# One hybrid decoder block on one core: token tile 0 runs ahead of tiles 1 to 3, tile 1 also gathers its rows of u, and the dense u products come before the dense v products

## The chip, the core and the metric

The kernel runs on one core of a Trainium2 chip. A core has five engines with separate instruction queues: PE (TensorE, matrix multiplies and transposes), DVE (VectorE), ACT (ScalarE), POOL (GpSimd) and SP (SyncE, which issues DMAs here). Sixteen DMA engines move data between HBM and the on-chip memory SBUF; matrix products land in the accumulators of PSUM (eight banks). The metric is the time of one execution on the device, in microseconds, as the median of several runs.

## What is computed

One layer for 512 tokens of width 2048, in float32. Cut to what matters:

```python
z = rmsnorm(x) @ w_in                       # 2048 -> about 6150 columns
att = forgetting_attention(...)             # 8 heads x 128, causal
cell = mlstm_chunkwise(...)                 # 4 heads, chunks of 128 tokens, state carried on
x = x + concat(headnorm(att), headnorm(cell)) @ w_out
# PEER, for each token:
q = rmsnorm(x) @ w_q                        # 8 heads x 2 halves x 128
scores = q . keys                           # 8 heads x 2 x 128 keys
idx, gate = top 16 of the 16 x 16 sums of the two halves' top 16, softmax   # of 16384 experts
act = gelu(u[idx] . x) * gate               # 128 rows of u for each token
x = x + sum over the 128 of act * v[idx]
out = rmsnorm(x)
```

The attention and the mLSTM are causal: the mixer of the first 128 tokens needs nothing of the later ones.

## The kernel before

The tokens are four tiles of 128 (P). Weights come from HBM in **chunks** of 128x1024 float32 (512 KB). `stream_split` (L101) loads a chunk into one of three `raw` buffers, ACT casts it into a `hi` part (L109) and DVE forms the remainder `lo` (L111); a `raw` buffer is free once `lo` is formed. A float32 product is three matmuls: hi by hi, hi by lo, lo by hi.

`project_nat` (L118) has 128 tokens as the stationary operand and 512 weight columns moving; `project_t` (L136) has 128 weight columns stationary and all tokens moving, 512 of them in the mixer. So a chunk serves 24 matmuls of 512 columns for four tiles. The order is: norm of all four tiles, mixer of all four tiles (`mlstm_pair`, `fox_pair`, both over `range(NT)`), `w_out` for tiles 0 and 1, then for tiles 2 and 3, with tile 0's norm, queries (`w_q0`, 256 columns moving) and expert choice as steps beside them.

Then PEER has two paths. **Tile 0 gathers**: for each of its 128 slots (8 heads by 16), an indirect DMA on POOL's queue (L588) brings one row of u for each token, 128x2048 (1 MB), into one of three `row` buffers, and one DVE instruction forms the dot product (L603, called a dot below); after the activation, 128 more gathers bring rows of v, which DVE adds up (L614). `advance(n)` moves this series on by n steps at the places where it is written; each gather also waits for the last `hi` cast traced before it, so it is spread over the kernel. **Tiles 1 to 3 are dense**: for every one of 128 blocks of 128 experts (two chunks of `uT`), `dense_steps` forms gelu(u x) for 384 tokens (`sacc`, 48 matmuls of 384 columns), and for 16 groups of 8 blocks the products with v are summed (`y`, 512 columns moving). Gates enter as a table [block, key, token] that is built 32 tokens at a time (L878 to L901: DVE forms one-hot rows `o`, PE multiplies them into `gp`, ACT copies them into `stg`, and a DMA stores them in `gtab`); `load_gates` reads one group of all twelve tables, and `gated` (L938) multiplies and splits into `wbuf`.

68 of the u blocks (NEARLY) run beside the expert choice and the tables, with their results stored in `stab`; the other 60 are formed in the v stage, between v groups. Instructions stand on each engine in an order that a scheduler fixes from the written order and priorities; every engine works through its own queue in that order, so an instruction that waits holds up all behind it on its engine.

Of the kernel before, what the change touches and what calls it, by code (L numbers as in the profile page):

```python
# [10 lines left out]
F32 = mybir.dt.float32  # L11
# [70 lines left out]
def block_kernel(ctx: ExitStack, tc: tile.TileContext, a, out):  # L82
    nc = tc.nc

    const = ctx.enter_context(tc.tile_pool(name="const", bufs=1))
    stream = ctx.enter_context(tc.tile_pool(name="stream", bufs=2))
    cst = const.tile([P, C_KEEP], F32, name="cst")
# [30 lines left out]
    def project_nat(psA, src, parts, hook=None):  # L118
        """[tokens, 512 columns] of part.T @ w, one bank for each token tile."""
        acc = [psA.tile([P, 512], F32, tag="acc", name="acc") for _ in parts]  # L120
        for s in range(8):
            hi, lo = stream_split(src[s])
            for j, part in enumerate(parts):
                for kk in range(2):
                    kc = 2 * s + kk
                    xh, xl = part[:, 0, kc, :], part[:, 1, kc, :]
                    wh = hi[:, kk * 512:(kk + 1) * 512]
                    wl = lo[:, kk * 512:(kk + 1) * 512]
                    mm(acc[j], xh, wh, kc == 0, False)
                    mm(acc[j], xh, wl, False, False)  # L130
                    mm(acc[j], xl, wh, False, kc == KC - 1)
            if hook:
                hook()
        return acc

    def project_t(psA, src, xT):  # L136
        """[256 columns, tokens] of w.T @ xT, one bank for each 128 columns."""
        acc = [psA.tile([P, 512], F32, tag="acc", name="acc") for _ in range(2)]
        for s in range(4):
            hi, lo = stream_split(src[s])  # L140
            for j in range(2):
                for kk in range(4):
                    kc = 4 * s + kk
                    wh = hi[:, kk * 256 + j * P:kk * 256 + (j + 1) * P]
                    wl = lo[:, kk * 256 + j * P:kk * 256 + (j + 1) * P]
                    mm(acc[j], wh, xT[:, 0, kc, :], kc == 0, False)
                    mm(acc[j], wh, xT[:, 1, kc, :], False, False)
                    mm(acc[j], wl, xT[:, 0, kc, :], False, kc == KC - 1)
        return acc
# [15 lines left out]
    def transpose_split(psB, src, dst, groups=range(4)):  # L165
        """src [128 tokens, 2048] -> dst [128, hi/lo, kc, tokens]."""
        for g in groups:
            pt = psB.tile([P, 4, P], F32, tag="ps", name="pt")
            for k in range(4):
                kc = 4 * g + k  # L170
                nc.tensor.transpose(pt[:, k, :], src[:, kc * P:(kc + 1) * P], ident)
            h = dst[:, 0, 4 * g:4 * g + 4, :]
            nc.scalar.copy(out=h, in_=pt)  # L173
            nc.vector.tensor_tensor(out=dst[:, 1, 4 * g:4 * g + 4, :], in0=pt, in1=h.bitcast(F32), op=OP.subtract)

# [1 line left out]
    ssq = const.tile([P, NT, 4], F32, name="ssq")  # L177

    def add_block(sq, acc, t, n):
        """x2 block += acc, and its sum of squares."""  # L180
        xs = x2[:, t, n * 512:(n + 1) * 512]
        nc.vector.tensor_tensor(out=xs, in0=acc, in1=xs, op=OP.add)
        nc.scalar.activation(out=sq, in_=xs, func=AF.Square, accum_out=ssq[:, t, n:n + 1])

    def rstd_x2(pool, t):
        ss = pool.tile([P, 1], F32, tag="ss", name="ss", bufs=4)
        nc.vector.tensor_reduce(out=ss, in_=ssq[:, t, :], axis=AX.X, op=OP.add)
        return rstd_of(pool, ss, D, 1)

# [5 lines left out]
    with ExitStack() as mx:  # L195
        mc = mx.enter_context(tc.tile_pool(name="mc", bufs=1))
        xT = xtp.tile([P, 2, KC, S], F32R, name="xT")
        parts = [xT[:, :, :, t * P:(t + 1) * P] for t in range(NT)]
        with tc.tile_pool(name="n1", bufs=2) as n1:
# [14 lines left out]
            for t in range(NT):  # L214
# [7 lines left out]
                transpose_split(psB, hn, parts[t])  # L222
        cm = mc.tile([P, C_WID - C_MQK], F32, name="cm")
        nc.sync.dma_start(out=cm, in_=a["consts"][:, C_MQK:])
        bd = cm[:, C_BD - C_MQK:C_BD - C_MQK + S].rearrange("p (h t) -> p h t", h=MH)
        maskb = mc.tile([P, 3 * P], BF16, name="maskb")
        nc.vector.tensor_copy(out=maskb[:, 0:P], in_=ident)
        nc.vector.tensor_copy(out=maskb[:, P:], in_=cm[:, 0:2 * P])
        identb, mqkb, mstb = maskb[:, 0:P], maskb[:, P:2 * P], maskb[:, 2 * P:3 * P]
# [4 lines left out]

        mp = mx.enter_context(tc.tile_pool(name="mp", bufs=1))
        sp = mx.enter_context(tc.tile_pool(name="sp", bufs=2))
        mixed = x2

        # gates in rows: 0..7 fox forget, 32..35 mlstm input, 64..67 mlstm forget
        cF = mp.tile([104, S], F32R, name="cF")  # L240
        bF = mp.tile([104, S], F32, name="bF")
        erow = mp.tile([36, S], F32, name="erow")
        negM = mp.tile([36, S], F32, name="negM")
        cols = mp.tile([P, NT, 100], F32, name="cols")
        def gate_rows():
            # x2 is free until the mixer's first heads: 16 slots of 512 columns
# [5 lines left out]

            gps = psB.tile([P, 512], F32, tag="ps", name="gps")
            for s in range(2):
                ghi, glo = stream_split(a["w_gate"][s], 8 * 96)
                for kk in range(8):
                    kc = 8 * s + kk
                    wh, wl = ghi[:, kk * 96:(kk + 1) * 96], glo[:, kk * 96:(kk + 1) * 96]
                    mm(gps[:96], wh, xT[:, 0, kc, :], kc == 0, False)
                    mm(gps[:96], wh, xT[:, 1, kc, :], False, False)  # L260
                    mm(gps[:96], wl, xT[:, 0, kc, :], False, kc == KC - 1)
            g = slot(96, S)
            nc.scalar.activation(out=g, in_=gps[:96], func=AF.Identity, bias=gbias)
# [7 lines left out]
            # log1p(ex) = ln(u) + (ex - (u - 1)) / u  # L271
# [11 lines left out]
            # fox: F = cumsum(log_sigmoid), in two parts in rows 0.. and 32.. of cF, with ones in  # L283
            # rows 64.. and 96..; bF has ones against the parts and -F against the ones
# [8 lines left out]
            nc.vector.tensor_copy(out=bF, in_=cm[0:104, C_BASEF - C_MQK:C_BASEF - C_MQK + S])  # L293
# [16 lines left out]
            # running maximum M of e (from the state's), m = b + M  # L310
# [25 lines left out]
        def gate_cols(rowx, ones4, mprev, Mr):  # L336
            # columns: 0.. exp(-m), 32.. exp(m_prev - M), 64.. exp(e - M_last), 96.. exp(m_prev - M_last)
# [14 lines left out]
        qkp = mx.enter_context(tc.tile_pool(name="qkp", bufs=2))  # L352

        def w2k(shape, name):
            return sp.tile(shape, F32, tag="w2k", name=name, bufs=6)

        def w1k(shape, name):
            return sp.tile(shape, F32, tag="w1k", name=name, bufs=5)

        def col1(name):  # L360
            return sp.tile([P, 1], F32, tag=name, name=name)

# [1 line left out]
        def mlstm_pair(p2):  # L364
            qk = []
            for w in range(2):
                acc = project_t(psA, a["w_mqk"][p2][w], xT)
                dst = qkp.tile([P, 2, S], F32, tag="qk%d" % w, name="mqk")
                for j in range(2):
                    ci = w * 4 + p2 * 2 + j  # L370
                    cin = w2k([P, S + 3], "cin")
                    nc.vector.memset(cin[:, 0:3], 0.0)
# [694 lines left out]
```

## Time and profile before

| | |
|---|---|
| three runs | 3295.75, 3298.84 (median), 3302.25 us |
| profiled execution, first to last instruction | 3298.2 us |
| PE busy | 3245.6 us (98%) |
| DVE busy | 2293.9 us (70%) |
| ACT busy | 1242.8 us (38%) |
| POOL busy | 473.8 us (14%) |
| moved by DMA | 751.69 MB, mean 228 GB/s |

The profile is of one execution whose span is 0.6 us under the median. An engine's busy time is the union of its instructions' intervals. Matmuls are pipelined: one lasts longer than the distance to the next one's start, so what a series of them costs is read from the distance of their starts in the timeline, not from the mean duration.

### The profile page before, as it was taken

The numbers are of one execution on the slowest core, as the hardware profiler recorded it, in microseconds if no ns is written. First come the engines' busy times: TensorE is split into PE (matmuls) and PEld (weight loads), VectorE is DVE, ScalarE is ACT, GpSimd is POOL, SyncE is SP. The second block draws the span as 40 slices with busy tenths as digits, with TensorE's granted clock in tenths as the row PEclk, the third lists the DMA queues.
The fourth block names the chain that finished last, engine by engine and source line by source line (L and its number), as shares of the span: only waits on it lengthen the run. The fifth ranks groups of instructions, "written<-read, shape, count | busy, mean of one in ns | idle before, by whom it ended". The sixth has DMA issues, their size and how long they took to land.

```text
span 3298.2 us, 43394 instructions
## 1 busy us (share of the span) xinstructions
PE 3245.6 (98%) x16681; PEld 2886.8 (88%) x16681; DVE 2293.9 (70%) x3746; ACT 1242.8 (38%) x1667; POOL 473.8 (14%) x380
## 2 busy tenths in 40 slices
PE   8999999999999999999999999999999999999998
PEld 6788787778799999999998888888899899898997
DVE  5542324467888989988867778876777767677774
ACT  4432223355554444455533333333233233232333
POOL 0000000100112323200012211111211112122110
PEclk9999999999999999999999999999999999999999
DMA  4232232266657667676788888887787887777774
GB/s 149 77 90 83 77 96 71 84 228 198 218 166 250 232 244 259 231 252 223 252 319 301 309 302 300 314 307 273 277 287 272 295 283 272 281 279 273 283 269 140
DMA packets 194065, 751.69 MB, mean 228 GB/s; under 512 B 19265, under 2 KB 61505, under 8 KB 158145
## 3 DMA queue, kind: packets, MB, share of 16 engines
q1 hardware_dynamic: 156994, 480.47, 41.8%
q0 software_dynamic: 36864, 268.45, 22.8%
q8 instruction: 131, 2.15, 0.3%
q14 instruction: 76, 0.62, 0.1%
HBM read 706.12 MB, written 42.73 MB: 227 GB/s over the span
## 4 chain that ended last, share of the span: by engine, by line
PE 73%; DMA 8%; issue 8%; DVE 7%; POOL 2%; ACT 1%; POOLq 0%; DVEq 0%; SPq 0%; ACTq 0%
PE y L116 24%; PE acc L116 22%; PE sacc L116 21%; DMA row<-in_u,idx 3%; DMA row<-in_v,idx 2%; DVE lo L111 2%; POOL row L588 2%; DMA raw<-in_w_out 1%; DVE x L614 1%; DMA stab<-es 1%; DMA raw<-in_uT 1%; PE sps L116 1%; ACT hi L109 1%; PE po L116 1%; DVE row L603 1%
## 5 line engine op out<-in xcount | busy, mean ns | idle before, releaser
L109 ACT CAST hi<-raw 128x1024 fp32r<-128x1024 f32 x736 | 773.8, 1052 | 1525.7 <-PE y L116 505.3
L111 DVE TENSOR_TENSOR lo<-raw,hi 128x1024 fp32r<-128x1024 f32 x736 | 900.6, 1227 | 514.4 <-ACT hi L109 513.3
L116 PE MATMUL sacc<-x3d,hi 128*128 128x384 f32 x4096 | 1052.7, 337 | 0.4 <-ACT x3d L173 0.4
L116 PE MATMUL y<-hi,wbuf 128*128 128x512 f32 x3048 | 942.0, 390 | 0.0
L116 PEld LDWEIGHTS sacc<-x3d,hi 128*128 128x128 f32 x4096 | 735.1, 188 | 1.2 <-ACT x3d L173 0.6
L116 PE MATMUL sacc<-x3d,lo 128*128 128x384 f32 x2048 | 686.0, 335 | 1.9 <-DVE lo L111 1.9
L116 PEld LDWEIGHTS y<-hi,wbuf 128*128 128x128 f32 x3048 | 572.9, 188 | 118.8
L116 PE MATMUL y<-lo,wbuf 128*128 128x512 f32 x1524 | 594.4, 390 | 5.2 <-DVE lo L111 5.0
L614 DVE SCALAR_TENSOR_TENSOR x<-row,act,x 128x2048 f32<-128x2048 f32 x128 | 300.9, 2351 | 138.3 <-DMA row<-in_v,idx 137.2
L116 PEld LDWEIGHTS sacc<-x3d,lo 128*128 128x128 f32 x2048 | 385.0, 188 | 4.4 <-DVE lo L111 4.4
L603 DVE SCALAR_TENSOR_TENSOR row<-row,x 128x2048 f32<-128x2048 f32 x128 | 293.8, 2295 | 120.3 <-DMA row<-in_u,idx 120.2
L116 PEld LDWEIGHTS y<-lo,wbuf 128*128 128x128 f32 x1524 | 286.4, 188 | 67.1 <-DVE lo L111 7.9
L588 POOL DMA_INDIRECT row<-in_u,idx x128 | 196.4, 1534 | 822.7 <-ACT hi L109 377.8
L588 POOL DMA_INDIRECT row<-in_v,idx x128 | 182.4, 1425 | 778.3 <-ACT hi L109 673.5
L116 PE MATMUL acc<-xT,hi 128*128 128x512 f32 x768 | 243.8, 395 | 0.0
L116 PE MATMUL acc<-hi,xT 128*128 128x512 f32 x768 | 241.8, 393 | 0.0
L116 PEld LDWEIGHTS acc<-hi,xT 128*128 128x128 f32 x768 | 143.8, 188 | 28.5
L116 PEld LDWEIGHTS acc<-xT,hi 128*128 128x128 f32 x768 | 143.7, 189 | 28.4 <-ACT xT L173 0.3
L116 PE MATMUL acc<-lo,xT 128*128 128x512 f32 x384 | 151.1, 393 | 0.0
L116 PE MATMUL acc<-xT,lo 128*128 128x512 f32 x384 | 150.4, 392 | 0.0
L156 POOL TENSOR_TENSOR rsr<-rst,mhalf 128x1 f32<-128x1 f32 (+2 forms) x24 | 19.0, 795 | 838.5 <-DVE rst L153 735.6
L893 DVE TENSOR_SCALAR o<-cst,i0T,gT 128x128 f32<-128x128 f32 x384 | 113.8, 345 | 35.5 <-PE gp__12799 L116 1.3
(522 smaller groups left out, 3073.6 us busy)
## 6 DMA issues: line engine op xcount, KB each, us to landing
raw<-in_uT SPq DMA_DIRECT2D x256, 512.0 KB, 5.0
raw<-in_vS SPq DMA_DIRECT2D x256, 512.0 KB, 5.1
raw<-in_w_out SPq DMA_DIRECT2D x64, 512.0 KB, 4.3
raw<-in_w_q SPq DMA_DIRECT2D x64, 512.0 KB, 4.5
gtab<-stg SPq DMA_DIRECT2D x12, 2048.0 KB, 7.5
gt<-gtab SPq DMA_DIRECT2D x16, 1536.0 KB, 9.8
raw<-in_w_fqk SPq DMA_DIRECT2D x32, 512.0 KB, 3.6
stab<-es SPq DMA_DIRECT2D x68, 192.0 KB, 4.4
```

The source lines that it names most:

```text
L109: pace[0] = nc.scalar.copy(out=hi[:, :width], in_=raw[:, :width]).ins
L111: nc.vector.tensor_tensor(out=lo[:, :width], in0=raw[:, :width], in1=hi[:, :width].bitcast(F32), op=OP.subtract)
L116: nc.tensor.matmul(out=o, lhsT=l, rhs=r, start=start, stop=stop)
L156: nc.gpsimd.tensor_tensor(out=r, in0=t, in1=mhalf[:, 0:width], op=OP.pow)
L588: ins = nc.gpsimd.indirect_dma_start(out=row, out_offset=None, in_=a[src], in_offset=bass.IndirectOffsetOnAxis(ap=idx0[:, j:j + 1], axis=0))
L603: nc.vector.scalar_tensor_tensor(out=row, in0=row, scalar=1.0, in1=x30, op0=OP.mult, op1=OP.mult, accum_out=dots[:, j - LAG:j - LAG + 1])
L614: nc.vector.scalar_tensor_tensor(out=x2[:, 0, :], in0=row, scalar=act0[:, j - LAG:j - LAG + 1], in1=x2[:, 0, :], op0=OP.mult, op1=OP.add)
L893: nc.vector.tensor_scalar(out=o0, in0=iota, scalar1=i0T[:, t:t + 1], scalar2=gT[:, t:t + 1], op0=OP.is_equal, op1=OP.mult)
```

## The change

- **Order.** The mixer runs for tile 0 alone first (`z_first`: 96 chunks of w_in, one token tile wide), then for tiles 1 to 3, which load the same 96 chunks again. Tile 0's `w_out`, norm, queries and expert choice (`rest_first`) are steps in a hook behind each chunk of the second pass, up to four of its own chunks at a time; from the 32nd hook on, the hook calls `advance` and the gathers begin.
- **Gathers.** One series: 128 gathers of u for tile 0, 128 of u for tile 1 (new), 128 of v for tile 0, with two steps of lag at each end. Tile 1's activations, times their gates, go into its gate table, so its four tables (of twelve) can be built only after its last dot.
- **Dense u** is over 256 tokens (tiles 2 and 3) for all 128 blocks, all ahead of the v stage; the results of all 128 go through `stab`. The v products stay over three tiles.
- **Counts of advance.** By the written paces, 182 steps of the series stand before the 117th u block; the rest of the u steps stand in one loop behind the 116th.
- The descriptor space of the gathers is halved (`dynamic_dma_scratch_size=8192`).

```diff
-ND = (NT - 1) * P       # tokens of the dense path (token tiles 1..3)
+TD = (NT - 1) * P
+TU = 2 * P
...
-NEARLY = 68             # expert blocks whose u products run beside the expert choice
...
+PACE_U = 0.9
+HOLD = 12
...
+    gathers = itertools.chain(u_rows(0), u_rows(1), v_rows())
...
+    LAST_U = 2 * (PH * TK + LAG)
...
+    def first_chunks(ps, src, x0, n):
...
+            yield 1
...
+            while going[0] and n < FIRST_CHUNKS:
+                step = next(rest, 0)
+                going[0] = step != 0
+                n += FIRST_CHUNKS if step == 2 else 1
+            if not going[0]:
+                advance(PACE_MIX)
...
+        acc = psA.tile([P, 512], F32, tag="acc", name="sacc")[:, 0:TU]
...
-        while nearly[0] < NEARLY:
+        while nearly[0] < NI - HOLD:
             early_s()
-            advance(PACE_G)
+            advance(PACE_U if done[0] < LAST_U else 0.0)
+        while done[0] < LAST_U + 1:
+            advance(1.0)
+        turn(gT, lambda t: gate[1], range(1, 2))
+        for tg in range(NT1):
+            k = min(EARLY_G, NI - nearly[0])
+            table(tg, itertools.chain(*[early_steps() for _ in range(k)]))
+        while nearly[0] < NI:
+            early_s()
```

The order on the engines at three places. PE at the last gate tables: before, the four matmuls of a table piece (`gp`) stand between products of dense u (`sacc`).

```order
L116 MATMUL sacc<-x3d,hi 128x384 x2
L116 MATMUL sacc<-x3d,lo 128x384
L116 MATMUL gp__15148<-o_15151,o_15149 128x128
L116 MATMUL gp__15148<-o_15154,o_15149 128x128
L116 MATMUL gp__15148<-o_15157,o_15149 128x128
L116 MATMUL gp__15148<-o_15160,o_15149 128x128
L116 MATMUL sacc<-x3d,hi 128x384 x2
```

PE at tile 1's tables in the changed kernel: the last product of dense u, the transpose of tile 1's gates, and then table pieces only (128 matmuls) up to the first v product (`y`).

```order
L139 MATMUL sacc<-x3d,hi 128x256 x2
L139 MATMUL sacc<-x3d,lo 128x256
L978 MATMUL pt<-cst,gate_86 128x128
L139 MATMUL gp<-o_20214,o_20212 128x128
L139 MATMUL gp<-o_20217,o_20212 128x128
```

```order
L139 MATMUL gp<-o_21465,o_21457 128x128
L139 MATMUL gp<-o_21468,o_21457 128x128
L139 MATMUL y<-hi,wbuf 128x512
L139 MATMUL y<-lo,wbuf 128x512
```

All 128 u blocks have moved ahead of the transpose, those too that are written behind it. On DVE before, dots stand singly between the splits of chunks (`lo`), here at the end of the tables.

```order
L111 TENSOR_TENSOR lo<-raw,hi 128x1024
L603 SCALAR_TENSOR_TENSOR row,dots<-row,x_4827 128x2048
L111 TENSOR_TENSOR lo<-raw,hi 128x1024 x3
L603 SCALAR_TENSOR_TENSOR row,dots<-row,x_4827 128x2048
L111 TENSOR_TENSOR lo<-raw,hi 128x1024 x2
L603 SCALAR_TENSOR_TENSOR row,dots<-row,x_4827 128x2048
```

DVE in the changed kernel, at the end of dense u: the fourth `lo` from below here is that of the last u chunk, and the three behind it are the first three of v.

```order
L320 SCALAR_TENSOR_TENSOR row,dots<-row,x_77 128x2048
L134 TENSOR_TENSOR lo<-raw,hi 128x1024
L320 SCALAR_TENSOR_TENSOR row,dots<-row,x_77 128x2048
L134 TENSOR_TENSOR lo<-raw,hi 128x1024
L320 SCALAR_TENSOR_TENSOR row,dots<-row,x_77 128x2048 x2
L134 TENSOR_TENSOR lo<-raw,hi 128x1024
L320 SCALAR_TENSOR_TENSOR row,dots<-row,x_77 128x2048
L134 TENSOR_TENSOR lo<-raw,hi 128x1024
L320 SCALAR_TENSOR_TENSOR row,dots<-row,x_77 128x2048 x47
L324 TENSOR_TENSOR gate_86<-dots,gate_86 128x128
```

Of tile 1's 128 dots, 51 now stand behind the last split of u (1, 2, 1 and 47), and 27 stand one or two at a time between the splits of the last 24 u chunks.

## Rows read from the trace of the kernel before

**Rows 1.** The page: span and busy time by engine

```profile
span 3298.2 us, 43394 instructions
PE 3245.6 (98%) x16681; PEld 2886.8 (88%) x16681; DVE 2293.9 (70%) x3746; ACT 1242.8 (38%) x1667; POOL 473.8 (14%) x380
```

**Rows 2.** Timeline of PE, three stretches: start, duration, instruction; moving columns 256, 384, 512

```profile
789.81 0.28 PE L116 MATMUL acc<-lo,x30T 128*128 128x256 f32 x1
...
790.17 0.28 PE L116 MATMUL acc<-lo,x30T 128*128 128x256 f32 x1
...
1656.50 1.05 PE L116 MATMUL gp__15119<-o,o 128*128 128x128 f32 x8
...
1671.11 0.33 PE L116 MATMUL sacc<-x3d,lo 128*128 128x384 f32 x1
1671.29 0.51 PE L116 MATMUL sacc<-x3d,hi 128*128 128x384 f32 x2
1671.63 0.33 PE L116 MATMUL sacc<-x3d,lo 128*128 128x384 f32 x1
...
2149.62 0.39 PE L116 MATMUL y<-lo,wbuf 128*128 128x512 f32 x1
...
2150.30 0.39 PE L116 MATMUL y<-lo,wbuf 128*128 128x512 f32 x1
```

**Rows 3.** Busy time in stretches: instructions in brackets, granted clock, DMA share, GB/s

```profile
30.00:660.00 630.00, 626.25 (x2894) 502.43 (x2893) 259.01 (x499) 203.84 (x370) 9.31 (x8) 1.00 0.28 85
785.00:805.00 20.00, 20.00 (x121) 17.83 (x120) 12.02 (x11) 11.23 (x15) 0.00 (x0) 1.00 0.79 241
960.00:1360.00 400.00, 393.22 (x2269) 388.10 (x2269) 355.35 (x1012) 176.11 (x242) 116.35 (x110) 1.00 0.68 238
1670.00:1750.00 80.00, 79.37 (x437) 76.06 (x436) 50.05 (x54) 25.82 (x36) 15.36 (x10) 1.00 0.96 354
1750.00:2240.00 490.00, 488.07 (x2152) 403.38 (x2151) 386.31 (x445) 151.96 (x176) 101.97 (x60) 1.00 0.84 301
```

**Rows 4.** DMA issues by line: count, KB each, median us from issue to landing

```profile
raw<-in_uT SPq DMA_DIRECT2D x256, 512.0 KB, 5.0
gtab<-stg SPq DMA_DIRECT2D x12, 2048.0 KB, 7.5
gt<-gtab SPq DMA_DIRECT2D x16, 1536.0 KB, 9.8
raw<-in_w_fqk SPq DMA_DIRECT2D x32, 512.0 KB, 3.6
```

**Rows 5.** Timeline of DVE in the table stage, with a dot

```profile
1385.27 0.69 DVE L887 TENSOR_TENSOR o<-cst,i1T 128x512 f32<-128x512 f32 x1
1385.87 1.11 DVE L893 TENSOR_SCALAR o<-cst,i0T,gT 128x128 f32<-128x128 f32 x4
1387.02 0.69 DVE L887 TENSOR_TENSOR o<-cst,i1T 128x512 f32<-128x512 f32 x1
...
1392.10 2.28 DVE L603 SCALAR_TENSOR_TENSOR row<-row,x 128x2048 f32<-128x2048 f32 x1
```

**Rows 6.** Groups of DVE within 960 to 1360 us: count, busy us, mean ns

```profile
L111 DVE TENSOR_TENSOR lo<-raw,hi 128x1024 fp32r<-128x1024 f32 x90 | 111.9, 1254 | 11.7 <-ACT hi L109 11.7
L603 DVE SCALAR_TENSOR_TENSOR row<-row,x 128x2048 f32<-128x2048 f32 x40 | 91.9, 2298 | 33.0 <-DMA row<-in_u,idx 32.9
L708 DVE SCALAR_TENSOR_TENSOR oh<-oh,it 128x256 f32<-128x256 f32 x46 | 22.7, 533 | 1.7 <-POOL oh L705 1.7
```

**Rows 7.** The two splits of a chunk over the whole run, from the page's groups

```profile
L109 ACT CAST hi<-raw 128x1024 fp32r<-128x1024 f32 x736 | 773.8, 1052 | 1525.7 <-PE y L116 505.3
L111 DVE TENSOR_TENSOR lo<-raw,hi 128x1024 fp32r<-128x1024 f32 x736 | 900.6, 1227 | 514.4 <-ACT hi L109 513.3
```

**Rows 8.** The gathered rows: issue on POOL, and issue to landing

```profile
L588 POOL DMA_INDIRECT row<-in_u,idx x128: 933/1279/3037, 975.7 to 2242.8; - x128
DMA to landing us min/median/max: 5.4/7.0/13.3
```

More of the change, by code (lines that the diff above doesn't have):

```diff
@@ new lines, in take, with gather @@
+    def take(t, i0, i1, g):
+        nc.vector.scalar_tensor_tensor(out=idx[t], in0=i0, scalar=128.0, in1=i1,
+                                       op0=OP.mult, op1=OP.add)
+        if g is not None:
+            nc.vector.tensor_copy(out=gate[t], in_=g)
+    late = {}
+    def gather(src, t, j):
+        row = rows.tile([P, D], F32, tag="row", name="row")
+        ins = nc.gpsimd.indirect_dma_start(
+            out=row, out_offset=None, in_=a[src],
+            in_offset=bass.IndirectOffsetOnAxis(ap=idx[t][:, j:j + 1], axis=0))
+        tc.add_manual_dep(ins.ins, pace[0].name,
+                          mybir.DependencyInfo(mybir.DependencyClass.Sync,
+                                               mybir.DependencyReason.DATA), reason="pace")
+        return row
@@ new lines, in gathered, with u_rows, dot @@
+    def gathered(src, t, use):
+        ahead = []
+        for j in range(PH * TK + LAG):
+            if j < PH * TK:
+                ahead.append(gather(src, t, j))
+            if j >= LAG:
+                use(ahead.pop(0), j - LAG)
+            yield
+    def u_rows(t):
+        def dot(row, j):
+            nc.vector.scalar_tensor_tensor(out=row, in0=row, scalar=1.0, in1=x2[:, t, :],
+                                           op0=OP.mult, op1=OP.mult, accum_out=dots[:, j:j + 1])
+        yield from gathered("u", t, dot)
+        nc.scalar.activation(out=dots, in_=dots, func=AF.Gelu)
+        nc.vector.tensor_tensor(out=gate[t], in0=dots, in1=gate[t], op=OP.mult)
+        nc.sync.dma_start(out=x2[:, t, :], in_=xs[t])
@@ new lines, in v_rows, with add @@
+    def v_rows():
+        def add(row, j):
+            nc.vector.scalar_tensor_tensor(out=x2[:, 0, :], in0=row, scalar=gate[0][:, j:j + 1],
+                                           in1=x2[:, 0, :], op0=OP.mult, op1=OP.add)
+        yield from gathered("v", 0, add)
+        junk = rows.tile([P, D], F32, tag="row", name="junk")
+        ss = late["fin"].tile([P, 1], F32, tag="ss", name="ss", bufs=4)
+        nc.scalar.activation(out=junk, in_=x2[:, 0, :], func=AF.Square, accum_out=ss)
+        late["norm"](0, rstd_of(late["fin"], ss, D, 1))
+        yield
@@ L195, in block_kernel @@
     with ExitStack() as mx:
[L196 to L199, printed above, removed]
+        xT = xtp.tile([P, 2, KC, TD], F32R, name="xT")
+        x0 = row_pair("x0T")
+        with ExitStack() as nx:
+            n1 = tpool(nx, "n1", 2)
             xi = [x2[:, t, :] for t in range(NT)]
@@ L458, in fox_pair @@
[L458 to L466 removed]
+        qkp = tpool(mx, "qkp", 2)
@@ L499, in block_kernel @@
[L499 to L513 removed]
+                na = psB.tile([P, 512], F32, tag="ps", name="na")
@@ new lines, in fox_pair @@
+        def fox_pair(p2, fv):
+            acc = project_t(psA, a["w_fqk"][p2][0], xT, hook)
+            fq = qkp.tile([P, 2, TD], F32, tag="qk0", name="fq")
+            for j in range(2):
+                nc.scalar.mul(out=fq[:, j, :], in_=acc[j], mul=float(P) ** -0.5)
+            acc = project_t(psA, a["w_fqk"][p2][1], xT, hook)
+            fk = qkp.tile([P, 2, TD], F32, tag="qk1", name="fk")
+            for j in range(2):
+                nc.scalar.copy(out=fk[:, j, :], in_=acc[j])
+            for j in range(2):
+                h = 2 * p2 + j
+                rF = fox_row(h, S)
+                for i in tiles:
+                    fox_tile(h, i, fq[:, j, (i - 1) * P:i * P], fk[:, j, :], fv, rF)
@@ new lines, in block_kernel @@
+        mlstm_pair(0)
+        mlstm_pair(1)
+        for g2 in range(2):
+            acc = project_nat(psA, a["w_fv"][g2], xT, tiles, hook)
+            fv = qkp.tile([P, NT - 1, 512], F32, tag="v", name="fv")
+            for j in range(NT - 1):
+                nc.scalar.copy(out=fv[:, j, :], in_=acc[j])
+            fox_pair(2 * g2, fv)
+            fox_pair(2 * g2 + 1, fv)
+        while going[0]:
+            hook()
+        wm = [qkp.tile([P, D // 2], F32, tag="v", name="wm") for _ in range(2)]
@@ new lines, in block_kernel @@
+        xtx.close()
+        xdp = ctx.enter_context(ExitStack())
+        x3d = tpool(xdp, "xdp", side="right").tile([P, 2, KC, TD], F32R, name="x3d")
+        parts = [[x3d[:, p, :, (t - 1) * P:t * P] for p in range(2)] for t in tiles]
+        for gs in (range(0, 3), range(3, 4)):
+            for t in tiles:
+                transpose_split(psB, mixed[:, t, :], *parts[t - 1], gs)
+    tp = tpool(ph, "tp")
+    sels = [tp.tile([P, NT - 1, PH, TK], F32, name=nm) for nm in ("i0f", "i1f", "gts")]
@@ L640, in early_steps @@
         nearly[0] += 1
-        sv = rows.tile([P, ND], F32, tag="row", name="es")
-        yield from dense_steps(psA, "acc", b, sv)
+        acc = psA.tile([P, 512], F32, tag="acc", name="sacc")[:, 0:TU]
+        for s in range(2):
+            w = stream_split(a["uT"][b, s])
+            for kk in range(8):
+                kc = 8 * s + kk
+                mm3(acc, [p[:, kk * P:(kk + 1) * P] for p in w],
+                    [x3d[:, p, kc, P:TD] for p in range(2)], kc == 0, kc == KC - 1)
+                if kc % 2 == 1 and kc < KC - 1:
+                    yield
+        sv = tp.tile([P, TU], F32, tag="es", name="es", bufs=3)
+        nc.scalar.activation(out=sv, in_=acc, func=AF.Gelu)
         nc.sync.dma_start(out=stab[b], in_=sv)
+        yield
     def early_s():
@@ new lines, in block_kernel, with alloc, dst, wq_hook @@
+    with ExitStack() as rx:
+        n2 = tpool(rx, "n2", 2)
+        sc23 = n2.tile([P, 2, PH, 2, P], F32, name="sc23", bufs=1)
+        def alloc(name, shape, dtype=F32):
+            return n2.tile(shape, dtype, tag=name, name=name)
+        def dst(t, h):
+            return [x[:, t - 1, h, :] for x in sels]
+        def wq_hook():
+            advance(PACE_WQ)
+        for h in range(PH):
+            acc = project_t(psA, a["w_q"][h], x3d, wq_hook)
+            qT = n2.tile([P, 2, TD], F32, tag="qT", name="qT", bufs=1)
+            for j in range(2):
+                nc.scalar.copy(out=qT[:, j, :], in_=acc[j])
@@ L857, in block_kernel @@
-        for h in range(PH):
-            scs = w_q(h)
-            for t in range(1, NT):
-                for _ in range(EARLY_TOPK[t - 1]):
+                scs = n2.tile([P, 2, P], F32, tag="scs", name="scs") if t == 1 else sc23[:, t - 2, h]
+                nc.scalar.copy(out=scs, in_=sc)
+                if t == 1:
+                    one = choose(alloc, scs, dst(1, h))
+            for _ in one:
+                pass
+        take(1, *[x[:, 0].rearrange("p h k -> p (h k)") for x in sels])
@@ L957, in block_kernel @@
     for g in range(NI // GB):
-        for blk in range(made, GB):
-            gated(g, blk, gt)
+        for s in range(made, GB // 2):
+            gated(g, s, gt)
         made = 0
@@ L962, in block_kernel @@
         if last:
-            for _ in sparse:
+            for _ in gathers:
                 pass
```

1025 lines of the change are left out of this document (499 added, 526 removed).

## Prediction

> **What bounds the kernel now.** I read the page first [rows 1]: PE is busy for 3245.6 of 3298.2 us, so the kernel ends when PE has worked through its queue, and there is little to win but work taken off PE. Then the timeline of PE, for what a matmul costs in a series [rows 2]: three of them (hi, lo, hi) take 790.17 − 789.81 = 0.36 us with 256 moving columns, 1671.63 − 1671.11 = 0.52 with 384 and 2150.30 − 2149.62 = 0.68 with 512, so 0.12, 0.173 and 0.227 us each. Then the busy time by stretch [rows 3]: in the mixer PE is busy for 626.25 of 630 us at 85 GB/s, beside the expert choice for 393.22 of 400 with DVE at 355.35, and in the v stage for 488.07 of 490 at 301 GB/s. PE is fed everywhere, because something dense always stands beside what waits. The question is whether the changed order still does that.
>
> The profiled span is 3298.2 us, 0.6 under the median of the runs; the sum is made against the span.
>
> **What PE gains.** Dense u has 128 blocks of 48 matmuls, 6144, at 256 columns for 384: 6144 x (0.173 − 0.12) = −326 us. The projections with stationary weights (1152 matmuls) go from 512 columns to 384 for tiles 1 to 3, 1152 x 0.054 = −62, and tile 0 adds 576 of 256 columns, +69. Those with stationary tokens only move. The gates are split into 48 matmuls of 384 and 48 of 128, +3. Sum on PE: **−316 us**. A doubt is that no row shows 256 columns with `uT` as the stationary side; the 256-column row has x30T there, loads its weights as often, and I take it. The v products keep their 4608 matmuls; per 16 chunks the stage moves little more than before, where PE was full at 301 GB/s [rows 3], so v costs nothing new.
>
> **What hides it no longer: the end of dense u.** By the order, 182 of the 260 gather steps of u precede block 117, and 51 dots of tile 1 stand on DVE behind the last split of u. No matmul is left for PE: the next one transposes tile 1's gates, which need all the dots; then come four tables, and the first v product needs them all. Price of the 51: the row buffers are three; a gather takes 5.4 us to land at best, 7.0 in the middle [rows 8], the dot 2.3 [rows 6], so a buffer turns in 8 to 9.5 us, a third of it is 2.7 to 3.2; and 1.05 MB at the 354 GB/s of the fullest stretch [rows 3] is 2.96. I take 3.0: **+153 us** (121 if DVE alone sets the pace at 2.3 and its handover, 200 at 3.9 with landings as slow as beside full loads). A page of the Trainium skill would put it lower: DMA: Bandwidth & Descriptors, section on the anatomy of one DMA, fits such a DMA as 2.0 us plus its bytes at 436 GB/s, 4.4 us for 1 MB. By that, an estimate, a buffer turns in 7 us, DVE would set the pace, and this term would be 121 for 153 and the time some 32 us less. The trace disagrees: no row landed in under 5.4 us [rows 8].
>
> The four tables then stand bare: 32 pieces of DVE at 1.75 us (1387.02 − 1385.27 [rows 5]) = 56, the store of a table 7.5 and the load of a group 9.8 [rows 4], the activation, transpose, last copy and first gating some 7; less the 128 table matmuls that PE had to do anyway, 128 x 0.13 = 17 [rows 2]: **+63** (50 to 90).
>
> In the last 12 blocks (24 chunks) the splits queue on DVE behind 27 dots, one to one, and a dot waits for its row. 24 x 0.524 + 12 x 0.13 + 27 x 1.05 = 42.5 MB at 354 GB/s is 120 us, for 69 us of PE: **+51** (20 to 90). In the 44 blocks before, 0.9 gathers stand beside each: 1.05 + 0.13 + 0.94 = 2.12 MB, 6.0 us at 354 GB/s against 5.76 of PE: **+13** (0 to 40).
>
> **What hides it no longer: the start.** `z_first` runs 98 chunks that serve one token tile: 12 matmuls of 256 columns (1.44 us) or 6 of 512 (1.36). A chunk's buffer turns in 3.6 (landing) [rows 4] + 1.05 + 1.23 [rows 7] = 5.9 us and three handovers, so three buffers give one chunk in about 2.1; the densest stream before, 241 GB/s for 20 us, is 9.2 chunks, 2.17 us each, with PE still full [rows 3]. 98 x 2.15 = 211 us, for 134 of these matmuls, 12 of gates and some 15 of attention and mLSTM: **+50** (0, were the loads as fast as PE, to 94 at 2.6). In 16 of the hooks that follow, five chunks share 9.75 us of PE and need 10.5 to 11, and eight expert choices of tile 0 fall on DVE there: **+25** (0 to 40).
>
> **What DVE and the queues take.** DVE gains 96 splits and 128 dots. In the stretch of 400 us that chooses experts it did 90 splits at 1.14, 40 dots at 2.3 and 23.5 choices in 355.35 us [rows 3, 6], so a choice is some 6.8. In the new order the 16 choices of tiles 2 and 3 stand within the first 73 u chunks with some 16 dots: 83 + 109 + 37 = 229 us, against 73 x 2.88 = 210 on PE. The eight tables of these tiles: 112 + 55 + 21 = 188 against 171. DVE is first in both; were it busy for 90% as before, the two would cost 86, if it ran full 36: I take **+45** (0 to 86). In the attention of tiles 1 to 3, where before no gathers ran, a dot of 2.3 us now stands before some of the short steps that PE waits for: **+15** (0 to 40). Between the mixer, `w_out` and the queries of tiles 1 to 3, norms and transposes of three tiles have no tile 0 work beside them any more; per tile 2.6 us of norm and as much of splits: **+15** (5 to 30). The waits on POOL's queue change nothing: choices stood between gathers there before.
>
> **Sum.** −316 + 153 + 63 + 51 + 13 + 50 + 25 + 45 + 15 + 15 = +114; 3298.2 + 114 = 3412 on the span, 3413 as a median. I forecast **3412 us**, slower. Bytes agree that it isn't fanciful: 752 + 50 (chunks loaded twice) + 134 (rows) + 11 (stab and copies) = 947 MB over 3412 us is 278 GB/s.
>
> **The rivals.**
>
> *Only the hole costs: faster.* If the three buffers for raw, hi and lo keep PE fed in every stage as they did before (97 to 100% [rows 3]), then only the 51 gathers and the tables remain: 3298 − 316 + 153 + 63 = 3198. For it: before, DVE at 89% left PE at 98%. Against: the chunk stream of the start, and dots that hold up splits, are set by counts that no buffer changes. It decides if the PE waits outside the hole sum to less than about 100 us; I have 214. Together with its milder forms that end under 3292: 0.13.
>
> *Gathers are slower than 3.0 us.* If a free-running series turns at 3.9 (landings of 9 us, since three rows and the loads crowd each other), the hole is 46 longer, the last 12 blocks 39 and the 44 before 27: 3524. For it: landings of up to 13.3 us [rows 8]. Against: 354 GB/s was held for 80 us. Over 3490: 0.09.
>
> *Narrow u products don't get faster.* With weight loads as the limit, dense u stays at 0.173: 3738. Against: 0.12 with a weight load for each [rows 2]. 0.02, within the last.
>
> **How the numbers follow.** Forecast, 3330 to 3490: 0.68. Between 3305 and 3330, most terms at their lower ends: 0.07. Within 0.2% (3292 to 3305; about what a measurement of this kernel can tell from no change): 0.03. Faster: 0.13. Above 3490: 0.09. So faster 0.13, same 0.03, slower 0.84. The range, 3290 to 3490, leaves 0.13 below and 0.09 above, near the two in ten.
>
> **What would show it.** Starts of `sacc` matmuls 0.12 us apart; one stretch of some 150 us behind the last `sacc` with PE idle, DVE at 70 to 80%, dots about 3.0 apart and little but row traffic, and 80 us more with 32 table pieces; then a v stage of some 1050 us with PE full. At the start, 96 chunks about 2.15 us apart with PE at three quarters, and `sacc` beginning about 1050 to 1080 us from the start. The prediction is wrong if PE is above 95% outside the hole, if the hole is under 180 us, or if dense u runs at another pace.

## The result and the profile after

The changed kernel takes 3609.19 us (median of 4 runs, 3587.95 to 3614.03) against 3297.3 (3291.49 to 3302.25): a ratio of 1.0936, with a 95% interval of 1.0903 to 1.0969. The forecast was slower, 3412, with a range up to 3490: the sign is right, the size is not. The cost is 312 us where 114 were forecast.

The page after, the lines that answer to [rows 1], with PE and its granted clock by fortieths of the span:

```profile
span 3611.3 us, 46307 instructions
PE 3094.8 (86%) x17377; PEld 2702.2 (75%) x17377; DVE 2673.0 (74%) x4219; ACT 1325.2 (37%) x1868; POOL 683.1 (19%) x508
...
PE   7879989998898998899988875027999999999999
...
PEclk7989999999999999999999997568999999999999
```

PE's share fell from 98% to 86%, in the hole and in nearly every stage besides. The busy time by stretch, the answer to [rows 3] (busy us with instructions in brackets of PE, PEld, DVE, ACT, POOL; then granted clock, DMA share, GB/s): `z_first`; the mixer of tiles 1 to 3; `w_out`; `w_q`; dense u up to the first table piece and from there to the last `sacc`; the hole; tile 1's tables; v.

```profile
44.00:302.00 258.00, 195.19 (x1007) 155.65 (x1005) 159.61 (x265) 140.40 (x210) 2.36 (x2) 0.89 0.61 190
302.00:954.00 652.00, 595.42 (x3142) 514.97 (x3141) 487.46 (x861) 260.21 (x421) 135.77 (x100) 0.98 0.68 243
954.00:1139.00 185.00, 152.37 (x664) 123.97 (x662) 147.27 (x163) 57.34 (x91) 50.01 (x37) 0.92 0.84 315
1139.00:1286.00 147.00, 146.84 (x870) 143.94 (x869) 125.98 (x320) 51.14 (x86) 36.37 (x36) 1.00 0.59 215
1286.00:1618.00 332.00, 294.12 (x2342) 290.47 (x2340) 266.71 (x749) 165.53 (x220) 65.39 (x68) 0.96 0.66 229
1618.00:2233.00 615.00, 544.52 (x4329) 535.82 (x4329) 458.14 (x627) 255.34 (x301) 118.55 (x77) 0.96 0.83 309
2233.00:2409.00 176.00, 0.52 (x5) 0.31 (x3) 119.28 (x106) 2.59 (x4) 74.70 (x50) 0.51 0.86 314
2409.00:2481.00 72.00, 39.83 (x258) 34.90 (x258) 58.28 (x163) 34.49 (x36) 0.94 (x1) 0.83 0.52 200
2481.00:3611.00 1130.00, 1092.06 (x4608) 875.67 (x4608) 820.98 (x913) 334.78 (x470) 196.66 (x129) 0.98 0.76 272
```

To set this against the forecast's terms I counted, in each stretch of both traces, every matmul at the pitch of its shape in an undisturbed series ("content"); what is left of the stretch is "rest". PE's content fell from 3202.5 to 2890.7 us, **−312** (forecast −316). The rest grew from 96 to 720:

| stretch after | length | content | rest | rest before | grew by | forecast |
|---|---|---|---|---|---|---|
| before `z_first` | 44 | 25 | 19 | 17 | 2 | 0 |
| `z_first` | 258 | 153 | 105 | none | 105 | 50 |
| mixer, `w_out`, `w_q` | 984 | 844 | 140 | 36 | 105 | 55 (25 + 15 + 15) |
| dense u | 947 | 796 | 152 | 24 | 127 | 109 (51 + 13 + 45) |
| hole and tile 1's tables | 248 | 29 | 219 | none | 219 | 216 (153 + 63) |
| v stage | 1130 | 1045 | 85 | 19 | 67 | 0 |

So the two terms that I had worked hardest on, PE's gain and the hole, came out within 4 us. That the hole came out is in part luck, as the section on the prediction shows. Of the 198 us that were missing, 190 are spread so: 67 in v, 55 in `z_first`, 50 in the mixer, 18 in dense u.

What PE waited for, over the whole run (us in total, times, longest):

```profile
PE pt L978 <- DVE gate L324: 175.6, 1, 175.6
PE sacc L139 <- DVE lo L134: 80.7, 44, 5.4
PE acc L139 <- DVE lo L134: 47.4, 56, 9.1
PE pp L639 <- ACT pr L634: 30.5, 18, 3.4
PE y L139 <- DVE lo L134: 28.4, 20, 3.3
```

One wait of 175.6 us is the hole. Next in size are the waits for the splits of chunks, which came late in every stage but `w_q` (there PE is busy for 146.84 of 147 us).

**The clock** belongs to that. A stretch in `z_first` behind an attention, in which PE waited time and again (0.4 to 2.0 us at a time), and PE's timeline within it:

```profile
189.50:199.00 9.50, 6.39 (x26) 5.61 (x27) 3.32 (x10) 2.95 (x10) 0.00 (x0) 0.50 0.42 122
```

```profile
196.05 0.63 PE L139 MATMUL acc<-hi,x0T 128*128 128x256 f32 x2
196.48 0.41 PE L139 MATMUL acc<-lo,x0T 128*128 128x256 f32 x1
196.69 0.63 PE L139 MATMUL acc<-hi,x0T 128*128 128x256 f32 x2
197.12 0.41 PE L139 MATMUL acc<-lo,x0T 128*128 128x256 f32 x1
```

The granted clock is 0.50, the lower level of 1.2 GHz, and three matmuls of 256 columns take 0.64 us (196.48 to 197.12) where they take 0.36 in [rows 2]. Summed over all matmuls that start at this level, the excess is 85 us, against 8 before: 77 of the 312 us are matmuls at the lower clock behind waits. I had priced every wait at its own length.

### The profile page after: what moved, and what is told of

Its sections match the earlier page's. It is cut to its first block, busy times and chain, and to the rows that moved or that the text cites. A ratio compares the mean times of both kernels' runs of the same rounds, so it can differ in the third digit from the quotient of the medians.

```text
span 3611.3 us, 46307 instructions
## 1 busy us (share of the span) xinstructions
PE 3094.8 (86%) x17377; PEld 2702.2 (75%) x17377; DVE 2673.0 (74%) x4219; ACT 1325.2 (37%) x1868; POOL 683.1 (19%) x508
## 4 chain that ended last, share of the span: by engine, by line
PE 34%; issue 24%; DMA 18%; DVE 15%; POOL 6%; ACT 3%; SPq 0%; POOLq 0%; DVEq 0%; ACTq 0%
PE y L139 19%; PE acc L139 8%; DMA row<-in_u,idx 6%; DVE lo L134 6%; POOL row L300 6%; DMA sv<-stab 5%; PE sacc L139 3%; ACT hi L132 2%; DMA row<-in_v,idx 1%; DMA raw<-in_w_out 1%; DVE o L996 1%; DMA raw<-in_w_mv 1%; DMA raw<-in_w_fqk 1%; DVE x L329 1%; PE gp L139 1%
## 5 line engine op out<-in xcount | busy, mean ns | idle before, releaser
L132 ACT CAST hi<-raw 128x1024 fp32r<-128x1024 f32 (+1 forms) x832 | 871.7, 1049 | 1556.7 <-PE y L139 364.1
L134 DVE TENSOR_TENSOR lo<-raw,hi 128x1024 fp32r<-128x1024 f32 (+1 forms) x832 | 1012.0, 1223 | 303.5 <-ACT hi L132 299.0
L320 DVE SCALAR_TENSOR_TENSOR row<-row,x 128x2048 f32<-128x2048 f32 x256 | 587.8, 2297 | 300.6 <-DMA row<-in_u,idx 300.2
L139 PE MATMUL sacc<-x3d,hi 128*128 128x256 f32 x4096 | 773.2, 290 | 21.5 <-ACT hi L132 21.5
L139 PE MATMUL sacc<-x3d,lo 128*128 128x256 f32 x2048 | 597.0, 292 | 81.0 <-DVE lo L134 80.7
L139 PE MATMUL y<-lo,wbuf 128*128 128x512 f32 x1524 | 610.1, 400 | 28.5 <-DVE lo L134 28.4
L300 POOL DMA_INDIRECT row<-in_u,idx x256 | 389.6, 1522 | 1123.3 <-ACT hi L132 882.3
L329 DVE SCALAR_TENSOR_TENSOR x<-row,gate,x 128x2048 f32<-128x2048 f32 x128 | 300.7, 2349 | 123.1 <-DMA row<-in_v,idx 122.6
L139 PE MATMUL acc<-xT,hi 128*128 128x384 f32 x768 | 199.8, 339 | 0.0
L139 PE MATMUL acc<-hi,x0T 128*128 128x256 f32 (+1 forms) x576 | 149.1, 346 | 3.9 <-ACT hi L132 3.7
L978 PE MATMUL pt<-cst,gate 128*128 128x128 f32 x1 | 0.4, 448 | 175.6 <-DVE gate L324 175.6
L139 PE MATMUL acc<-x3d,hi 128*128 128x384 f32 x512 | 132.8, 337 | 0.7 <-ACT x3d L211 0.7
```

Of the source, the lines that this page charges most:

```text
L132: pace[0] = nc.scalar.copy(out=hi[:, :width], in_=raw[:, :width]).ins
L134: nc.vector.tensor_tensor(out=lo[:, :width], in0=raw[:, :width], in1=hi[:, :width].bitcast(F32), op=OP.subtract)
L139: nc.tensor.matmul(out=o, lhsT=l, rhs=r, start=start, stop=stop)
L300: ins = nc.gpsimd.indirect_dma_start(out=row, out_offset=None, in_=a[src], in_offset=bass.IndirectOffsetOnAxis(ap=idx[t][:, j:j + 1], axis=0))
L320: nc.vector.scalar_tensor_tensor(out=row, in0=row, scalar=1.0, in1=x2[:, t, :], op0=OP.mult, op1=OP.mult, accum_out=dots[:, j:j + 1])
L329: nc.vector.scalar_tensor_tensor(out=x2[:, 0, :], in0=row, scalar=gate[0][:, j:j + 1], in1=x2[:, 0, :], op0=OP.mult, op1=OP.add)
```

## The experiments

Single runs are each set beside a run of the kernel before (3294.7 to 3298.4); stretches are read from the trace, and their lengths repeat within some 15 us where an edit doesn't touch them.

**e1: could the 51 rows stand earlier?**

```diff
-PACE_WQ = 0.5; PACE_C = 0.4; PACE_G = 0.4; PACE_U = 0.9
+PACE_WQ = 1.0; PACE_C = 1.0; PACE_G = 1.0; PACE_U = 1.35
```

> Paces raised (WQ 0.5 to 1.0, C 0.4 to 1.0, G 0.4 to 1.0, U 0.9 to 1.35), so that by the order nearly all 260 gather steps of u stand before the 117th u block. Theory A, the hole is only missing cover: the stretch from the last sacc to the tile 1 transpose falls from 176 us to under 25, the stretch from the first sacc (1286) to the last (2233) grows by no more than 60, time 3440 to 3500. Rival B, DVE and DMA have no room earlier: the 51 rows (51 x 2.3 us of DVE, 51 x 3.5 us as measured in the hole) come back as PE waits in the u stretch, which grows by 120 to 180; time 3580 to 3630.

3486.21 us. First `sacc` to first `y`, of e1 and of the changed kernel:

```profile
1314.00:2356.00 1042.00, 889.61 (x6926) 871.39 (x6924) 868.82 (x1616) 459.79 (x558) 249.60 (x182) 0.94 0.84 307
```

```profile
1286.00:2481.00 1195.00, 878.99 (x6931) 861.50 (x6929) 902.41 (x1641) 457.95 (x561) 259.57 (x196) 0.89 0.77 281
```

The transpose of tile 1's gates now stands at 2237 us, 100 us ahead of the last `sacc` (2336 us), so the tables are covered too. The stretch is 153 us shorter: of the 219 us of rest in hole and tables 48 came back as waits and slow clock in dense u, and 18.5 are left as the wait of the first `y` for its gates. 28 us are lost again before `sacc` starts (1314 for 1286). From first to last `sacc` it is now 1022 us for 947, 75 more, some 28 of them the matmuls of tile 1's tables, which stand there now; Theory A had allowed 60, Rival B wanted at least 120. With the time and the vanished hole that is Theory A: most of the hole was missing cover.

**e2: loads of `sv` earlier.** Their issue was written two steps ahead.

> Only the loads of stored u results in the v stage (sv) are issued two steps earlier. Theory A: the 90 us that DVE waits for sv (28 times) push back splits and gates and so cause PE's waits in the v stage: they fall under 20 us, and the v stage (first to last y) goes from 1121 us to 1080 to 1100. Rival B: the waits for gathered rows (123 us) or the slow y pitch of 0.232 are the cause: the v stage stays within 8 us of 1121.

3610.72 us; v from the first `y` to the end 1124 us for 1130, and 1115 from first to last `y`, within Rival B's 8 us of 1121. But it tells nothing on the loads: in SP's queue they stand where they stood, and DVE waits for them as long (84.8 us, 28 times). It serves as the base of e3.

**e3: the place of `wbuf`.** As e2, with a tile of 1408 bytes per partition allocated ahead of `wbuf`.

> As e2, and the stationary tile of the v products (wbuf) moved by 1408 bytes per partition, to the offset modulo 2048 that it had before the change. Theory A, the place of wbuf makes the 512-column pitch 0.232 for 0.227: the pitch in the v stage returns to 0.227, and the stage is 4608 x 0.0055 = 25 us shorter than e2's. Rival B, it is something else: pitch stays 0.232 and the stage agrees with e2's within 5 us.

3579.72 us. A series of v products in the changed kernel and in e3 (a `lo` row is one matmul, a `hi` row between two of them a pair):

```profile
2800.60 0.39 PE L139 MATMUL y<-lo,wbuf 128*128 128x512 f32 x1
2800.83 0.62 PE L139 MATMUL y<-hi,wbuf 128*128 128x512 f32 x2
2801.29 0.40 PE L139 MATMUL y<-lo,wbuf 128*128 128x512 f32 x1
2801.52 0.64 PE L139 MATMUL y<-hi,wbuf 128*128 128x512 f32 x2
2801.99 0.39 PE L139 MATMUL y<-lo,wbuf 128*128 128x512 f32 x1
```

```profile
2800.08 0.39 PE L139 MATMUL y<-lo,wbuf 128*128 128x512 f32 x1
2800.30 0.62 PE L139 MATMUL y<-hi,wbuf 128*128 128x512 f32 x2
2800.76 0.39 PE L139 MATMUL y<-lo,wbuf 128*128 128x512 f32 x1
2800.98 0.62 PE L139 MATMUL y<-hi,wbuf 128*128 128x512 f32 x2
2801.44 0.39 PE L139 MATMUL y<-lo,wbuf 128*128 128x512 f32 x1
```

Six matmuls take 1.39 us and 1.36 us. Over the stage the median pitch is 0.232 in the changed kernel, as in e2, and 0.227 in e3: 26 us of the 67 in v are this. The stage is only 16 us shorter than e2's, since waits and slow clock took 10 back; runs at 0.232 differ among themselves by about as much in this stage, so it is the pitch that tells, not the length. With `wbuf` at 928 modulo 2048 (e6) the pitch is 0.229, for which neither of my two rules was right, and at 992 (e5) 0.227. The tiles behind `wbuf` move with it, so that it is the place of `wbuf`, and not of a neighbour, is likely but not shown.

**e4: four buffers for raw chunks.** `bufs=3` becomes 4 for `raw`, the descriptor space 4096.

> Four raw buffers for chunks instead of three (the gathers' descriptor space is halved once more to make room). Theory A, the turn of three buffers sets the pace of z_first: its chunks come 1.6 to 1.75 us apart instead of 2.17 and z_first (44 to 302 us) takes 200 to 220 us instead of 258. Rival B, the stream of loads itself is the limit at about 240 GB/s: the pace stays at 2.1 to 2.2 and z_first at 250 to 260. Rival C, serial chains (attention, mLSTM) set it: chunk pace falls, but z_first stays above 240.

3553.55 us; `z_first` 230 us for 258, the median distance of its chunks 1.78 us for 2.5, and dense u 922 for 947. Between A and C: the buffers set the chunk's pace, and chains without chunks remain. The v stage takes 13 us more than in the changed kernel (1143 for 1130).

**e10: no attention of tile 0 in `z_first`.** The call of `fox_tile(h, 0, ...)` is left out.

> Leaves out the attention of tile 0 alone (8 heads in z_first; tile 0's half of the mixer's result is then wrong). Theory A, the chain of attention, in which no chunk is taken, costs z_first some 10 us in each of its four places: z_first falls from 258 us to 215 to 225. Rival B, the chunk loop of three raw buffers covers it: 245 to 258.

`z_first` takes 235 us, in the middle between A and B. The chain of waits of the changed kernel shows both parts (start, length; 65 longest pieces of 44 to 302 us):

```profile
163.02 1.24 DVE lo L134
164.28 4.25 DMA raw<-in_w_fqk
169.70 1.24 DVE lo L134
...
178.12 4.24 DMA raw<-in_w_fqk
183.54 1.24 DVE lo L134
184.82 1.59 PE acc L139 x11
187.79 1.23 DVE lo L134
190.28 1.23 DVE lo L134
195.83 4.49 PE acc L139 x24
```

A buffer turns in 6.7 us (163.02 to 169.70: landing 4.25, `hi`, `lo`), with three of them a chunk in 2.2. Then, from 184 to 200, the chain runs over PE and the attention, and no load of a chunk is on it. I had put attention and mLSTM into the sum as PE's work, 15 us. The attention's own matmuls are 5 us at their pitches; of the 23 us that e10 saves, the other 18 are rest, time in which the stream of chunks stands. The mLSTM's chains were not taken out by any run.

**e5, e6, e9: what slows dense u, rows or dots?** e5 leaves both of tile 1 out, e6 only the dots, e9 only the gathers.

> Leaves out tile 1's gathers of u and its dots (tile 1's activations are then not the reference's); tile 0's rows stay. Prices the whole of tile 1's rows. Theory A, the rows cause the waits of dense u: the 176 us behind the last sacc fall under 5, PE's waits and slow-clock time between the first table piece and the last sacc (106 us in 1618 to 2233) fall under 40, time 3330 to 3390. Rival B, DVE's splits and tables alone are too slow beside PE: those 106 us stay above 80, time 3400 to 3440. Beside it wbuf is moved by 128 bytes, to 992 modulo 2048: if the pitch goes by the place modulo 256, it is 0.227 here; if only the old place (224 modulo 2048) is fast, it stays 0.232.

> Tile 1's rows of u are gathered as before, but its dots on DVE are left out (its activations are then not the reference's). Theory A, a dot that waits for its row holds up the splits behind it on DVE: the 106 us of waits and slow clock between the first table piece and the last sacc fall under 40 as in e5. Rival B, the rows' traffic slows the chunks: they stay above 80. Beside it wbuf is moved by 64 bytes, to 928 modulo 2048 (160 modulo 256): 0.232 if the place modulo 256 decides, 0.227 if any other place than 864 is fast.

> The other half of e6: tile 1's dots stand on DVE (all 126 of them between the splits of the u chunks, 2.3 us each, on rows that are there already), and its gathers are left out (its activations are then not the reference's). Theory A, traffic of the rows slows dense u, not DVE's work: from the first table piece to the last sacc (615 us, with 106 us of waits and slow clock; 618 with 83 in e6; 545 with 11 in e5) it takes 545 to 570. Rival B, DVE's work is as much to blame: 590 to 640.

From the first table piece to the last `sacc`, in this order:

```profile
1610.00:2155.00 545.00, 542.50 (x4576) 542.35 (x4577) 354.39 (x638) 289.91 (x334) 3.62 (x2) 1.00 0.63 218
```

```profile
1611.00:2229.00 618.00, 562.01 (x4580) 554.92 (x4581) 350.31 (x636) 286.33 (x333) 130.68 (x90) 0.96 0.88 338
```

```profile
1619.00:2211.00 592.00, 546.37 (x4575) 545.27 (x4575) 579.64 (x855) 290.53 (x335) 4.07 (x2) 0.96 0.60 203
```

Set against PE's content (542 us in these three, with the matmuls of tile 1's tables; 515 in the changed kernel, 615 us long), the rest is 3 us in e5, 76 in e6 with 90 rows gathered in the stretch, 51 in e9 with 108 dots, and 100 in the changed kernel with 77 rows and 75 dots. Without both, PE is full at clock 1.00. Rows alone, with DVE busy for only 350 of 618 us, make chunks late by their traffic, 338 GB/s: ACT waits 203.0 us (80 times) for chunks to land in this stretch, and 5.9 us (3 times) in e5's. It isn't a price for each row: 48 rows in the first 464 us cost 23, the 42 in the last 154 us 52, where the DMA engines were busy all the time at 416 GB/s:

```profile
2075.00:2229.00 154.00, 112.73 (x870) 109.90 (x869) 83.11 (x184) 60.73 (x71) 44.89 (x42) 0.88 1.01 416
```

The 592 us of e9 lie in Rival B's range, but its trace doesn't bear Rival B out. The stretch up to 2066 us, the 50 us behind it, and PE's wait that ends them:

```profile
1619.00:2066.00 447.00, 444.83 (x3726) 444.20 (x3726) 445.60 (x624) 227.42 (x265) 0.00 (x0) 1.00 0.64 216
2066.00:2116.30 50.30, 6.89 (x58) 6.69 (x56) 50.30 (x47) 3.73 (x5) 2.27 (x1) 0.59 0.10 30
2116.35 0.58 PE L139 MATMUL sacc<-x3d,lo 128*128 128x256 f32 x1 [43.46 <-DVE lo L134]
```

In the first, 86 dots stand among the splits and tables and fill DVE for 445.60 of 447 us, and the rest is only 4. In the second, this run's order has 22 dots in a row ahead of one split, against what I had expected (dots between splits only), and PE waits 43.46 us for that split: 44 of the 51 are this one block. So rows by their traffic are shown as a cause, 75 us of rest where nobody reads them; dots that need not wait for a row are not, as long as they stand among splits. The changed kernel has 100 with fewer rows than e6. A dot that waits for its row holds up the splits behind it there (DVE waits 120.9 us for rows in this stretch, 52 times), and that may be what is left over; no run separates it.

e5 takes 3280.18 us, and 26 of its gain are the pitch (`wbuf` at 992). At 0.232 it would be at 3306: **even without any cost of tile 1's rows, narrower u products only pay for the new order** (one run; some of the work is left out in it).

**e7: no choices of tiles 2 and 3.** Copies stand for the 16 calls of `choose`.

> Leaves out the 16 expert choices of tiles 2 and 3 (copies stand in for them, so their experts are wrong). Theory A, choices make DVE the bound of the stretch from the last w_q product to the first table piece (332 us for 48 blocks of 5.76 us, 276): it falls to 280 to 300. Rival B, rows set it: 315 to 332.

Last `w_q` product to first table piece:

```profile
1293.00:1605.00 312.00, 288.72 (x2342) 285.68 (x2341) 163.24 (x179) 119.27 (x156) 29.52 (x20) 0.98 0.69 243
```

312 for 332 us, though DVE has 104 us less to do; the run takes 3581.76. That lies between A and B. Runs that leave this stretch's work nearly as it is took 320 to 332, so choices cost 8 to 20 us here, less than I had said. What makes up the 31 us of rest that stay is not shown; 17 rows are gathered there, and without tile 1's rows (e5) the stretch is 322.

**e11: no gathers beside the mixer and `w_out`.** `PACE_MIX = 0`.

> No gathers beside the mixer of tiles 1 to 3 and w_out (pace 0 there; the whole series moves back by 98 steps, so the hole gets longer by some 98 x 3.5 = 340 us; only the stretch up to w_q is read). Theory A, rows and dots cause that stretch's waits: 582 to 1139 us, 99 us of waits and slow clock beside gathers, falls by 50 to 70. Rival B, hooks, narrow chunks and the short chains of attention cause them: it falls by less than 25.

First chunk of the second pass to the first `w_q` product, in e11 and in the changed kernel:

```profile
303.00:1073.00 770.00, 729.75 (x3803) 628.88 (x3802) 424.71 (x827) 316.53 (x511) 35.15 (x39) 0.99 0.47 148
```

```profile
302.00:1139.00 837.00, 747.79 (x3804) 638.94 (x3802) 634.73 (x1023) 317.55 (x512) 185.79 (x137) 0.97 0.72 259
```

67 us less: Theory A. The run as a whole takes 3846.06 us, with a hole of 489. So beside the mixer, rows and dots cost 67 us, for which I had 15 (attention) and nothing beside `w_out`. In the attention, ACT waited 60 us for a maximum that DVE formed late:

```profile
ACT pr L634 <- DVE nm L632: 60.0, 20, 8.4
```

73 us of rest stay in e11's stretch, for 36 before the change up to the last `w_q` product; no run took the hooks or the narrow chunks out.

**e8, e12: paces, buffers and place together.**

> The raised paces of e1, the four raw buffers of e4 and the place of wbuf of e3 together. If the three causes are separate (123, 56 and 26 us), time is 3390 to 3420 and still slower than before; if they share waits, 3430 to 3480.

> The kernel of e8 again, timed against the kernel before: 3370 to 3400 us, ratio 1.02 to 1.035, still slower.

3383.95 us, and timed 3389.45 (3378.04 to 3400.79): a ratio of 1.0285 to the kernel before, interval 1.0244 to 1.0326. The three gains added up would give 3404 (123 + 56 + 26 from 3609), so the total is near their sum, but by luck: stage by stage they don't add. The pitch is 0.227, and yet v from the first `y` to the end is 1132 us for 1130, since PE's waits for splits went from 28.4 to 50.8 us there, and the slow clock's excess from 14 to 21:

```profile
PE y L139 <- DVE lo L134: 50.8, 17, 5.5
```

First `sacc` to first `y` takes 988 us for 1195, 207 less, where e1 alone gave 153, and `z_first` takes 230 as in e4. No version that does the whole work was faster than the kernel before.

## Why the prediction was wrong in size

The step that failed is the one from "something dense always stands beside what waits" to stages priced as if PE or the stream of chunks stayed full in them: v at nothing (measured 67), `z_first` at its loop's pace with attention and mLSTM as PE's work beside it (105 for 50), and the mixer with a few single terms (105 for 55). These are 172 of the 198 us. The rest of the sum held, in part by luck:

- **PE's gain** (−316): right, −312. The doubt about 256 columns with `uT` stationary is settled: `sacc` stands 0.12 us apart, and "narrow u products don't get faster" is out.
- **The hole** (+153) and **bare tables** (+63): 219 for 216, but two misses cancel. The hole was 176: a row took 3.50 us, not 3.0 (50 dots behind the last `sacc`, at 314 GB/s). The tables were 43: they took 72 us for 80, of which PE's own matmuls are 29 and not 17, since each of the 128 stands in the trace as two records (256 of them, 0.11 us apart), which the working "128 x 0.13" took for one. By the estimate from the page of the Trainium skill that I had cited (DMA: Bandwidth & Descriptors, the anatomy of one DMA) the hole would have been 121 us; the trace puts it at 176. In the row's timeline DVE still waits for the landing before each dot (0.92, 1.79, 0.63 us):

```profile
2298.38 2.29 DVE L320 SCALAR_TENSOR_TENSOR row<-row,x 128x2048 f32<-128x2048 f32 x1 [0.92 <-DMA row<-in_u,idx]
...
2302.47 2.29 DVE L320 SCALAR_TENSOR_TENSOR row<-row,x 128x2048 f32<-128x2048 f32 x1 [1.79 <-DMA row<-in_u,idx]
...
2305.40 2.29 DVE L320 SCALAR_TENSOR_TENSOR row<-row,x 128x2048 f32<-128x2048 f32 x1 [0.63 <-DMA row<-in_u,idx]
```

- **v costs nothing new** (0): the largest miss, 67 us. I compared the stage's products and bytes with a stretch where PE was full, and asked nothing else. 26 us are the pitch (e3); 13 are slow clock (14.0 for 1.5); some 24 are waits, nearly all for splits (28.4 us, 20 times, for 5.0 before), whose cause stays open: e2 was to show it and didn't. The first product's wait of 17 us for its gates stands ahead of the stage and is counted with the tables.
- **The start** (+50, at most 94): 105. A buffer that turns without a break gives a chunk in 2.2 us, as I had it (2.15), and e4 shows that three raw buffers are the cause. But the chunks came 2.5 us apart in the median, and the stage took 258 us where I had 211. What failed is the addition: attention and mLSTM were counted as PE's work beside the stream, and the attention stops it (18 of e10's 23 us); matmuls at the lower clock are 16 more in the stage, in part the same time. What remains of the 55 no run assigns.
- **Hooks, attention, transitions** (+55): 105. The dots that I priced at 15 in the attention cost 67 with their rows, `w_out` included (e11); hooks and transitions were not measured apart.
- **Dense u** (+51, +13, +45): 127 for 109. The size is near, the shares are not: I put 45 on choices and tables, and choices are 8 to 20 (e7). From the first table on, the rest is 100; rows alone make 76 of rest (e6), dots alone 4 outside one block (e9), and how much is the two together stays open.
- **The clock**: no term had it. 77 us lie across all of these.
- The mark "`sacc` begins about 1050 to 1080 us" didn't follow from my own sum: it left out the queries of tiles 1 to 3 (768 matmuls of 0.173 us, 133 us), which before stood among the u products. With them, and the +105 of the terms up to there, the sum gave 917 + 133 + 105 and some 10 of tile 0's own products, about 1165; it was 1286.
- **The range** ended at 3490, from the rival that rows turn at 3.9 us. It held no case in which several small terms lie at their upper ends together. The start went beyond its upper end (105, with 94 allowed), the mixer's terms came close to theirs (105, with 110), dense u stayed near its middle, and v had no upper end at all.

## What to carry to other kernels

A kernel whose slowest engine is 98% busy has that from what stands beside every wait; a change that takes work off the engine and also takes this cover away must be priced stage by stage as content plus rest, the rest from each stage's own loop and chain, for stages too in which the work seems unchanged. Small waits need not be independent: the same thin cover, the same traffic and a clock that falls behind waits can push several of them up together, and what one edit gives back in a stage, waits can take again (e8). Where work must wait for a late series, spread the series first: raising four pace constants gave 123 of the 312 us back.

## What the runs showed of the hardware

- Matmuls of 512 columns stood 0.232, 0.229 or 0.227 us apart in kernels that differ in where in a partition `wbuf` and the tiles behind it lie (`wbuf` at 864, 928, and 992 or 224 modulo 2048): 26 us over 4608 products. Nothing in the diff tells of it, since the allocator chose the place.
- Waits of PE of some tenths of a microsecond to a few at a time were followed by stretches at granted clock 0.50; the excess of the matmuls in them was 85 of the 720 us of rest.
- 90 gathered rows that no engine read, at 338 GB/s with the chunks, slowed a stretch of 545 us by 73, most of it where the DMA engines were busy all the time (416 GB/s).
- 86 dots of 2.3 us that kept DVE busy for 445.60 of 447 us beside dense u left 4 us of rest on PE; 22 of them in a row ahead of one split cost PE 43.46 us.
